# Gate and up by Strassen's scheme, down as a second phase, in an encoder block with two FFNs

## The chip, the cores and the metric

One core of one Trainium2 chip runs the whole kernel. Its time is the device time of one execution in microseconds (us), the median of several runs.

## The reference

One layer of a hybrid encoder over 1280 tokens (1024 of one request, 256 of another), width 1024:

```
x = x + 0.5 * post1(SwiGLU_1(pre1(x)))        # FFN 1
h = pre2(x);  p = h @ w_in
A = bidirectional RWKV-7(p);  B = grouped-query attention(p)
x = x + post2((sigmoid(gA)*(A @ w_branch_a) + sigmoid(gB)*(B @ w_branch_b)) @ w_out)
x = x + 0.5 * post3(SwiGLU_2(pre3(x)))        # FFN 2
swiglu(h) = (silu(h @ w_gate) * (h @ w_up)) @ w_down     # 1024 -> 2816 -> 1024
```

Every pre and post is an RMSNorm. The RWKV part has small low-rank (LoRA) projections for decay and gate, of 64 rows for each of two directions.

## The kernel before

Everything is kept with full-precision products: an operand is split into a high part (the value cast to the matmul's type) and a low part (the rest), and a product is three matmuls, high x high, high x low, low x high. `split` (L134) does this with one ScalarE cast (L140) and one VectorE subtraction (L141).

The stages in order: FFN 1, the combined projection with attention and the RWKV preparation, the RWKV loop, the two branch projections, the output projection (`gx2`, L1226), FFN 2.

An FFN runs in `ffn` (L169). `pre` (L98) has normalised the tokens, transposed them on TensorE (L121, L123) and split them into `hT`, in three chunks of 512, 512 and 256 tokens. For each of 22 blocks of 128 hidden columns, `wtile` (L143) loads the gate block (512 KB) and splits it, `projT` (L155, matmul L165) multiplies it with all chunks (24 matmuls a chunk: 8 depth steps by 3), ScalarE applies Silu (L178); the same for the up block, VectorE multiplies (L187) and the product is split. After two such blocks their part of the down projection is made: for each of 10 token tiles and 2 halves of the output, 6 matmuls (L206) into a PSUM bank, which VectorE adds to an accumulator `acc` in SBUF (L211; the first time ScalarE copies, L209). After the last block every tile goes through `post` (L289: a product with the gain on GpSimd, L293, the scale and residual on VectorE, L295).

A tile framework puts the instructions of each engine in an order of its own: it walks the program by priority (program order) and simulated times, gives out tile slots of each tag as they come free, and sets the semaphores. On the chip each engine then runs its own list in order. All DMAs are issued from SyncE's queue.

In the RWKV preparation `prep` (L562 on) makes, for each of 4 column groups, 5 chunks of 256 tokens and 2 directions, two pairs of matmuls (L576, L577): the high part of a LoRA weight at full height of 128 rows, and its low part at 64 rows, those of the direction.

Of the kernel before, what the change touches and what calls it, by code (L numbers as in the profile page):

```python
# [7 lines left out]
F32 = mybir.dt.float32  # L8
# [23 lines left out]
LT = 9  # L32
HK = 1
AH = (3, 3, 3)
FB = {"t5": 5, "d4": 6, "dg": 6}
DV = [(1, 4, 7), (3, 7, 9), ()]


class K:
# [57 lines left out]

    def pre(self, W, st, ps, gcol, get_x, ptag, ahead=AH, dve=(), weights=None, normed=False):  # L98

        nc = self.nc  # L100
        out, got = [], []
        for ci, (c0, n) in enumerate(CH):
            h = self.htile(ci)
            xs = []
            for t in range(c0 // 128, (c0 + n) // 128):
                while len(got) < min(TT, ORD.index(t) + 1 + ahead[ci]):
                    got.append(get_x(ORD[len(got)]))
                x = got[ORD.index(t)]
                if normed:
                    xs.append((x, None))  # L110
                    continue

                sq = W.tile([128, D], BF16, name="sq", tag="t5") if ORD.index(t) in dve else None
                dg = W.tile([128, 128], F32, name="dg", tag="dg")
                nc.scalar.activation(out=dg, in_=self.ident, func=AF.Copy, scale=self.rstd(st, x, dve=sq))
                xs.append((x, dg))
            for k in range(KD):
                p = ps.tile([128, 512], F32, name="ptr", tag=ptag)
                for j, (x, dg) in enumerate(xs):
                    if dg is None:  # L120
                        nc.tensor.transpose(p[:, j * 128:(j + 1) * 128], x[:, k * 128:(k + 1) * 128], self.ident)  # L121
                        continue
                    nc.tensor.matmul(p[:, j * 128:(j + 1) * 128], lhsT=x[:, k * 128:(k + 1) * 128], rhs=dg, start=True, stop=True)  # L123
                gk = self.par[:, gcol + k:gcol + k + 1]
                nc.scalar.activation(out=h[:, 0, k], in_=p[:, :n], func=AF.Copy, scale=gk)
                nc.vector.scalar_tensor_tensor(out=h[:, 1, k], in0=p[:, :n], scalar=gk, in1=h.bitcast(F32)[:, 0, k],
                                               op0=ALU.mult, op1=ALU.subtract)
            out.append(h)
            if weights is not None and ci == HK:

                self.ready = self.wtile(weights)
        return out

# [35 lines left out]
    def ffn(self, W, ps, hT, wgu, wd, acc, G=2):  # L169
        nc = self.nc  # L170
        group = []
        for f in range(NF):
            gh, gl = self.wtile(wgu[f, 0])
            sg = W.tile([128, NT], F32, name="sg", tag="t5")

            def eg(ci, p):
                c0, n = CH[ci]
                nc.scalar.activation(out=sg[:, c0:c0 + n], in_=p[:, :n], func=AF.Silu)  # L178
            self.projT(ps, gh, gl, hT, "gu", eg)
            uh, ul = self.wtile(wgu[f, 1])  # L180
            ah = W.tile([128, NT], F32R, name="ah", tag="t5")
            al = W.tile([128, NT], F32R, name="al", tag="t5")

            def eu(ci, p):
                c0, n = CH[ci]
                s = slice(c0, c0 + n)
                nc.vector.tensor_tensor(out=sg[:, s], in0=sg[:, s], in1=p[:, :n], op=ALU.mult)  # L187
                self.split(ah[:, s], al[:, s], sg[:, s])
            self.projT(ps, uh, ul, hT, "gu", eu)
            raw = W.tile([128, D], F32, name="draw", tag="d4")  # L190
            nc.sync.dma_start(out=raw, in_=wd[f * 128:(f + 1) * 128])
            dh = W.tile([128, D], F32R, name="dh", tag="d4")
            dl = W.tile([128, D], F32R, name="dl", tag="d4")
            self.split(dh, dl, raw)
            group.append((ah, al, dh, dl))
            if len(group) == G or f == NF - 1:
                first = f < G
                for t in ORD:
                    ts = slice(t * 128, t * 128 + 128)
                    for hf in range(2):  # L200
                        hs = slice(hf * 512, hf * 512 + 512)
                        p = ps.tile([128, 512], F32, name="pd", tag="dn")
                        i, m = 0, 3 * len(group)
                        for (a_h, a_l, d_h, d_l) in group:
                            for a, b in ((a_h, d_h), (a_h, d_l), (a_l, d_h)):
                                nc.tensor.matmul(p, lhsT=a[:, ts], rhs=b[:, hs], start=i == 0, stop=i == m - 1)  # L206
                                i += 1
                        if first:
                            nc.scalar.copy(acc[:, t, hs], p)  # L209
                        else:  # L210
                            nc.vector.tensor_tensor(out=acc[:, t, hs], in0=acc[:, t, hs], in1=p, op=ALU.add)  # L211
                group = []
        return acc
# [74 lines left out]

    def post(self, W, st, y, gbc, half, xres, late=False):  # L289

        nc = self.nc
        yg = W.tile([128, D], F32, name="yg", tag="d4")
        (nc.vector if late else nc.gpsimd).tensor_tensor(out=yg, in0=y, in1=gbc, op=ALU.mult)  # L293
        r = self.rstd(st, y, half)
        nc.vector.scalar_tensor_tensor(out=y, in0=yg, scalar=r, in1=xres, op0=ALU.mult, op1=ALU.add)  # L295
# [85 lines left out]
class Rwkv:  # L381
# [43 lines left out]
    def prep_weights(self, q, W):  # L425
# [9 lines left out]
        lo = W.tile([128, 2, 128], F32R, name="llo")  # L435
        for d in range(2):
            rs = slice(64 * d, 64 * d + 64)
            nc.vector.tensor_tensor(out=lo[rs], in0=raw[rs, d], in1=hi.bitcast(F32)[rs, d], op=ALU.subtract)
# [121 lines left out]
    def prep(self, q, got, ci, W, ps):  # L560
# [10 lines left out]
        for d in range(2):  # L571
            ds_ = slice(64 * d, 64 * d + 64)
# [485 lines left out]
def build(tc, I, O):  # L1058
    nc = tc.nc
    k = K(tc, I, O)  # L1060
    with tc.tile_pool(name="cst", bufs=1) as cp, tc.tile_pool(name="dr", bufs=1, space=DRAM) as dr, \
# [10 lines left out]
        xs = dr_tiles(dr)  # L1072

# [238 lines left out]
```

## Time and profile before

| what | value |
|---|---|
| median of 3 runs | 3557.58 us (3556.7 to 3557.88) |
| profiled execution | 3558.98 us, its span 3557.2 us |
| TensorE busy | 3467.9 us, 97% |
| VectorE, ScalarE, GpSimd busy | 48%, 36%, 11% |
| granted TensorE clock, mean | 0.988 |
| DMA, mean | 74 GB/s |

A profile line names line, engine, operation, `out<-in`, shape and count. TensorE's matmuls are pipelined: the time of one on a line is longer than the distance to the next, so the distance from start to start (the pitch) is what a matmul costs in a stream. A bracket at the end of a line says how long the engine was idle before it and what released it. Windows list busy times of the engines in a stretch, with the share of the clock that was granted, the share of DMA time in use, and GB/s.

### The profile page before, as it was taken

The numbers are of one execution on the slowest core, as the hardware profiler recorded it, in microseconds if no ns is written. First come the engines' busy times: TensorE is split into PE (matmuls) and PEld (weight loads), VectorE is DVE, ScalarE is ACT, GpSimd is POOL, SyncE is SP. The second block draws the span as 40 slices with busy tenths as digits, with TensorE's granted clock in tenths as the row PEclk, the third lists the DMA queues.
The fourth block names the chain that finished last, engine by engine and source line by source line (L and its number), as shares of the span: only waits on it lengthen the run. The fifth ranks groups of instructions, "written<-read, shape, count | busy, mean of one in ns | idle before, by whom it ended". The sixth has DMA issues, their size and how long they took to land. (4 is left out here: it accounts for less than half of the span.)

```text
span 3557.2 us, 56074 instructions
## 1 busy us (share of the span) xinstructions
PE 3467.9 (97%) x22608; PEld 2907.8 (82%) x22608; DVE 1720.8 (48%) x3300; ACT 1291.6 (36%) x2524; POOL 376.7 (11%) x706
## 2 busy tenths in 40 slices
PE   8999999999899999999989999998999999999997
PEld 7888888888788888887768888888878888888886
DVE  3233333333726776648777667647332333333335
ACT  4211111111523666746556666623432111111112
POOL 0000000000301000003144444410000000000002
PEclk9999999999999999999999999999999999999999
DMA  3111111111324121224352212147221111111103
GB/s 127 42 36 36 36 48 36 42 36 35 131 83 135 59 73 45 84 77 154 130 184 85 70 54 76 41 146 236 102 83 36 42 36 36 36 45 39 36 30 119
DMA packets 155108, 264.93 MB, mean 74 GB/s; under 512 B 16864, under 2 KB 98016, under 8 KB 154720
## 3 DMA queue, kind: packets, MB, share of 16 engines
q1 hardware_dynamic: 154848, 261.34, 22.9%
q8 instruction: 178, 2.92, 0.3%
q14 instruction: 82, 0.67, 0.1%
HBM read 183.94 MB, written 74.06 MB: 73 GB/s over the span
## 5 line engine op out<-in xcount | busy, mean ns | idle before, releaser
L165 PE MATMUL pp<-hT,whi 128*128 128x512 f32 (+1 forms) x6000 | 1643.1, 360 | 7.8 <-ACT qk L950 4.9
L165 PEld LDWEIGHTS pp<-hT,whi 128*128 128x128 f32 x6000 | 1068.0, 190 | 175.6 <-ACT qk L950 5.7
L165 PE MATMUL pp<-hT,wlo 128*128 128x512 f32 (+1 forms) x3000 | 1074.4, 358 | 0.0
L165 PEld LDWEIGHTS pp<-hT,wlo 128*128 128x128 f32 x3000 | 569.3, 190 | 79.8
L141 DVE TENSOR_TENSOR wlo<-wraw,whi 128x1024 fp32r<-128x1024 f32 x125 | 154.1, 1233 | 566.7 <-ACT whi L140 566.6
L211 DVE TENSOR_TENSOR acc<-acc,pd 128x512 f32<-128x512 f32 x400 | 271.3, 685 | 203.4 <-PE pd L206 203.2
L206 PE MATMUL pd<-dh,ah 128*128 128x512 f32 x880 | 346.4, 394 | 13.8 <-DVE acc L211 13.8
L206 PE MATMUL pd<-dh,al 128*128 128x512 f32 x880 | 345.6, 393 | 0.0
L206 PE MATMUL pd<-dl,ah 128*128 128x512 f32 x880 | 345.4, 392 | 0.0
L293 POOL TENSOR_TENSOR yg<-acc,gb 128x1024 f32<-128x1024 f32 x19 | 48.2, 2544 | 2075.1 <-DMA xb<-x_d 1128.6
L723 ACT CAST tt<-inv 128x512 f16<-128x512 f32 x400 | 226.6, 588 | 90.7 <-PE inv L721 66.4
L187 DVE TENSOR_TENSOR sg<-sg,pp 128x512 f32<-128x512 f32 x132 | 79.0, 598 | 347.8 <-PE pp L165 347.8
L140 ACT CAST dh<-draw 128x1024 fp32r<-128x1024 f32 x44 | 46.0, 1046 | 528.8 <-DMA draw<-wd 528.8
L140 ACT CAST ah<-sg 128x512 fp32r<-128x512 f32 x132 | 72.2, 547 | 439.5 <-DVE sg L187 439.5
L206 PEld LDWEIGHTS pd<-dh,ah 128*128 128x128 f32 x880 | 166.7, 189 | 52.0 <-DVE acc L211 18.1
L717 DVE TENSOR_TENSOR y<-inv,lv 128x256 f16<-128x256 f32 x400 | 161.6, 418 | 83.6 <-PE inv L715 61.4
L140 ACT CAST whi<-wraw 128x1024 fp32r<-128x1024 f32 x125 | 131.1, 1049 | 194.1 <-PE pp L165 191.7
L206 PEld LDWEIGHTS pd<-dh,al 128*128 128x128 f32 x880 | 166.7, 189 | 35.3
L206 PEld LDWEIGHTS pd<-dl,ah 128*128 128x128 f32 x880 | 166.6, 189 | 33.8
L178 ACT ACTIVATE sg<-pp 128x512 f32<-128x512 f32 x132 | 69.1, 524 | 327.1 <-PE pp L165 325.8
L1156 PE MATMUL pbr<-yT,whi 128*128 128x256 f32 x640 | 124.1, 291 | 19.2 <-ACT yT L140 8.9
L720 PE MATMUL inv<-y,tt 128*128 128x128 f16 x800 | 130.7, 221 | 0.0
(228 smaller groups left out, 4868.3 us busy)
## 6 DMA issues: line engine op xcount, KB each, us to landing
wraw<-wgu SPq DMA_DIRECT2D x88, 512.0 KB, 3.5
draw<-wd SPq DMA_DIRECT2D x44, 512.0 KB, 3.8
gate_d<-go SPq DMA_DIRECT2D x16, 640.0 KB, 3.2
ar_d<-ar SPq DMA_DIRECT2D x40, 256.0 KB, 2.1
bk_d<-bk SPq DMA_DIRECT2D x40, 256.0 KB, 2.1
AR<-ar_d SPq DMA_DIRECT2D x80, 128.0 KB, 2.9
BK<-bk_d SPq DMA_DIRECT2D x40, 256.0 KB, 2.9
g<-gate_d SPq DMA_DIRECT2D x80, 128.0 KB, 3.3
```

Of the source, the lines that this page charges most:

```text
L140: self.nc.scalar.copy(dst_h, src)
L141: self.nc.vector.tensor_tensor(out=dst_l, in0=src, in1=dst_h.bitcast(F32), op=ALU.subtract)
L165: nc.tensor.matmul(p[:, :n], lhsT=a[:, ks], rhs=h[:, b, k], start=i == 0, stop=i == 23)
L178: nc.scalar.activation(out=sg[:, c0:c0 + n], in_=p[:, :n], func=AF.Silu)
L187: nc.vector.tensor_tensor(out=sg[:, s], in0=sg[:, s], in1=p[:, :n], op=ALU.mult)
L206: nc.tensor.matmul(p, lhsT=a[:, ts], rhs=b[:, hs], start=i == 0, stop=i == m - 1)
L211: nc.vector.tensor_tensor(out=acc[:, t, hs], in0=acc[:, t, hs], in1=p, op=ALU.add)
L293: (nc.vector if late else nc.gpsimd).tensor_tensor(out=yg, in0=y, in1=gbc, op=ALU.mult)
L717: nc.vector.tensor_tensor(out=y1, in0=m, in1=mask(l), op=ALU.mult)
L720: nc.tensor.matmul(dbl[:, h, 0], lhsT=tt[:, h, 1], rhs=y1[:, h], start=True, stop=True)
L723: nc.scalar.copy(tt, dbl)
L1156: nc.tensor.matmul(p, lhsT=a[:, ks], rhs=ys[ci][:, b, kk], start=i == 0, stop=i == 11)
```

## The change

FFNs. Two hidden blocks f and f+1 (as rows of the transposed product) by the two halves of the depth form a 2x2 block matrix A, the tokens of the first two chunks by the two halves of the depth a 2x2 matrix B. `columns2` computes the four blocks of the product with 7 products of half depth instead of 8; the 256 tokens of the third chunk (`T`) are computed as before. `second_chunk` makes the combinations T1 to T4 of B once per FFN and splits them; S1 to S4 of A are made and split for each pair and each of gate and up. Operands are in a ring of 6 slots (`opr`). The product silu(gate)*up is written to DRAM (`a_d`). `down` then runs in three groups of tiles (4, 4 and 2), each with its accumulators in PSUM through all 22 blocks: for every block and group it loads the activations and both halves of the down weights again, and splits them. `ends` scales straight from PSUM, with no GpSimd. For the first pair, what needs no combination is done first for gate and up (`early`), with its four weight blocks loaded twice. In FFN 2 the output projection takes the tiles in the order of `PRE` and interleaves the first and third chunk's transposes.

LoRA. The low part of a weight is kept at 128 rows for each direction, the other 64 set to zero on GpSimd. The tile `go` moves to the tag `w1`, of which there are 3 slots.

```diff
-FB = {"t5": 5, "d4": 6, "dg": 6}
+FB = {"t5": 3, "w2": 8, "sc": 5, "x1": 2, "dg": 6}
+YB = {"y": 8, "op": 3}
+GRP = ((0, 1, 2, 3), (4, 5, 6, 7), (8, 9))
+PRE = (0, 1, 2, 3, 8, 9, 4, 5, 6, 7)
...
+    def second_chunk(self, W, ps, xs, gcol):
+        nc = self.nc
+        for k in range(4):
...
+            self.turn(p12, xs, k)
+            self.turn(p22, xs, k + 4)
...
+            o = self.slot("B22", k)
+            self.hilo(o[:, 0], o[:, 1], p22, g4)
+            b12 = W.tile([128, 512], F32, name="b12", tag="sc")
+            nc.scalar.activation(out=b12, in_=p12, func=AF.Copy, scale=g0)
+            t3 = W.tile([128, 512], F32, name="t3", tag="sc")
+            nc.vector.scalar_tensor_tensor(out=t3, in0=p22, scalar=g4, in1=b12, op0=ALU.mult, op1=ALU.subtract)
+            o = self.slot("T3", k)
+            self.split(o[:, 0], o[:, 1], t3)
+            o = self.slot("B11", k).bitcast(F32)
+            t1 = W.tile([128, 512], F32, name="t1", tag="sc")
+            nc.vector.tensor_tensor(out=t1, in0=o[:, 0], in1=o[:, 1], op=ALU.add)
+            nc.vector.tensor_tensor(out=t1, in0=b12, in1=t1, op=ALU.subtract)
...
+    def opr(self, src, n=512):
+        i = self.nop % len(self.ring)
+        self.nop += 1
+        pool, tag = self.ring[i]
+        o = pool.tile([128, 2, 512], F32R, name="op", tag=tag)
+        self.split(o[:, 0, :n], o[:, 1, :n], src)
+        return o
...
+    def prod(self, out, o, rhs, start, stop):
+        i = 0
+        for k in range(4):
+            ks = slice(k * 128, k * 128 + 128)
+            for a, b in ((0, 0), (0, 1), (1, 0)):
+                self.nc.tensor.matmul(out, lhsT=o[:, a, ks], rhs=rhs(k, b), start=start and i == 0, stop=stop and i == 11, skip_group_check=True)
+                i += 1
+    def columns2(self, W, ps, wgu, f, j, sg, hT, bank=None, early=False):
...
+        A = self.blocks(W, w, ("A11", "A12", "A21", "A22"))
+        o = self.opr(A["A11"])
+        self.prod(X, o, comb("B11"), True, True)
+        nc.scalar.copy(x1, X)
+        self.prod(T[:, :256], o, tail(0), True, False)
+        o = self.opr(A["A12"])
+        self.prod(T[:, :256], o, tail(1), False, True)
+        direct(0, slice(1024, NT), T[:, :256])
+        self.prod(X, o, comb("B21"), False, True)
+        direct(0, slice(0, 512), X)
+        o = self.opr(A["A21"])
+        self.prod(T[:, 256:], o, tail(0), True, False)
+        if early:
...
+            yield
+            A = self.blocks(W, w, ("A11", "A12", "A21", "A22"))
+        S = {n: W.tile([128, 512], F32, name="w2", tag="w2") for n in ("S1", "S2", "S3", "S4")}
...
+        self.prod(Y, self.opr(S["S2"]), comb("T2"), True, True)
+        nc.vector.tensor_tensor(out=u, in0=x1, in1=Y, op=ALU.add)
+        self.prod(Z, self.opr(S["S1"]), comb("T1"), True, True)
+        nc.scalar.copy(p5, Z)
+        self.prod(V, self.opr(S["S3"]), comb("T3"), True, True)
+        nc.vector.tensor_tensor(out=v, in0=u, in1=V, op=ALU.add)
+        self.prod(Z, self.opr(S["S4"]), comb("B22"), False, True)
+        nc.vector.tensor_tensor(out=c12, in0=u, in1=Z, op=ALU.add)
...
+        o = self.opr(A["A22"])
+        if not early:
+            self.prod(T[:, 256:], o, tail(1), False, True)
+            direct(1, slice(1024, NT), T[:, 256:])
+        self.prod(V, o, comb("T4"), False, True)
+        nc.vector.tensor_tensor(out=c22, in0=v, in1=p5, op=ALU.add)
+        nc.vector.tensor_tensor(out=c21, in0=u, in1=V, op=ALU.add)
...
+    def down(self, W, ps, wd, a_d, tiles):
+        nc, n = self.nc, 128 * len(tiles)
+        bk = [[ps.tile([128, 512], F32, name="pd", tag="mm") for _ in range(2)] for _ in tiles]
         for f in range(NF):
...
+            tag = ("w2", "sc")[f % 2]
+            ar = W.tile([128, 512], F32, name="ar", tag=tag)
+            nc.sync.dma_start(out=ar[:, :n], in_=a_d[f][:, tiles[0] * 128:tiles[0] * 128 + n])
+            a = self.opr(ar[:, :n], n)
+            d = []
+            for hf in range(2):
+                raw = W.tile([128, 512], F32, name="draw", tag=tag)
+                nc.sync.dma_start(out=raw, in_=wd[f * 128:(f + 1) * 128, hf * 512:hf * 512 + 512])
+                d.append(self.opr(raw))
+            for i in range(len(tiles)):
+                ts = slice(i * 128, i * 128 + 128)
+                for hf in range(2):
+                    for m, (x, y) in enumerate(((0, 0), (0, 1), (1, 0))):
+                        nc.tensor.matmul(bk[i][hf], lhsT=a[:, x, ts], rhs=d[hf][:, y], start=f == 0 and m == 0, stop=f == NF - 1 and m == 2)
+    def ends(self, W, WY, st, bk, tiles, gb, xres, put):
+        for i, t in enumerate(tiles):
+            y = WY.tile([128, D], F32, name="y", tag="y")
+            for hf in range(2):
+                hs = slice(hf * 512, hf * 512 + 512)
+                nc.vector.tensor_tensor(out=y[:, hs], in0=bk[i][hf], in1=gb[:, hs], op=ALU.mult)
+            ys.append((y, self.rstd(st, bk[i], True)))
+        for t, (y, r) in zip(tiles, ys):
...
+            nc.vector.scalar_tensor_tensor(out=y, in0=y, scalar=r, in1=x, op0=ALU.mult, op1=ALU.add)
+            nc.sync.dma_start(out=put(t), in_=y)
...
-        lo = W.tile([128, 2, 128], F32R, name="llo")
+        lo = W.tile([128, 2, 2, 128], F32R, name="llo")
...
-                nc.tensor.matmul(p[:, j], lhsT=lo[ds_, j], rhs=src[ds_, d, cs], start=False, stop=True)
+                nc.tensor.matmul(p[:, j], lhsT=lo[:, d, j], rhs=src[:, d, cs], start=False, stop=True)
...
-        o = W.tile([128, n], F32, name="go", tag="go")
+        o = W.tile([128, n], F32, name="go", tag="w1")
...
+                    for i, ts in enumerate(GRP):
+                        bk = k.down(W, ps, I["wd"][0], a_d, ts)
+                        if i == 2:
+                            norm2(1)
+                        y = k.ends(W, WY, st, bk, ts, gb, k.xin, lambda t: x1_d[t * 128:(t + 1) * 128])
+                        ys.update(zip(ts, y))
+                        if i == 1:
+                            norm2(0)
+                    k.ready = k.wtile(I["watt"][5])
+                    norm2(2)
```

`norm2` normalises and transposes a chunk of FFN 1's output for the projection that follows. `B11` and `B21` are the first chunk's halves, `B22` the second's lower half; `prod` is one product of half depth (12 matmuls).

## Rows read from the trace of the kernel before

**Rows 1.** Page, part 1: busy us, share of the span, instructions.
```profile
PE 3467.9 (97%) x22608; PEld 2907.8 (82%) x22608; DVE 1720.8 (48%) x3300; ACT 1291.6 (36%) x2524; POOL 376.7 (11%) x706
```

**Rows 2.** Windows, FFN 1's steady stretch: length, engines' busy us, clock, DMA share, GB/s.
```profile
200.00:800.00 600.00, 600.00 (x2976) 510.49 (x2975) 198.84 (x271) 90.99 (x134) 0.00 (x0) 1.00 0.12 39
```

**Rows 3.** Timeline of TensorE in both FFNs: start, us, line, count.
```profile
852.00 0.39 PE L206 MATMUL pd<-dl,ah 128*128 128x512 f32 x1
852.68 0.39 PE L206 MATMUL pd<-dl,ah 128*128 128x512 f32 x1
...
866.79 0.62 PE L165 MATMUL pp<-hT,whi 128*128 128x512 f32 x2
...
867.47 0.40 PE L165 MATMUL pp<-hT,whi 128*128 128x256 f32 x2
...
867.82 0.40 PE L165 MATMUL pp<-hT,whi 128*128 128x256 f32 x2
...
3500.04 0.63 PE L165 MATMUL pp<-hT,whi 128*128 128x512 f32 x2
...
3500.74 0.63 PE L165 MATMUL pp<-hT,whi 128*128 128x512 f32 x2
```

**Rows 4.** Groups by line and form, 0 to 870 us, VectorE and ScalarE.
```profile
L141 DVE TENSOR_TENSOR al<-sg,ah 128x512 fp32r<-128x512 f32 x40 | 27.7, 692 | 27.4 <-ACT ah L140 27.4
L126 DVE SCALAR_TENSOR_TENSOR hT<-ptr,par,hT 128x512 fp32r<-128x512 f32 x16 | 11.0, 744 | 3.8 <-ACT hT L125 3.8
...
L140 ACT CAST ah<-sg 128x512 fp32r<-128x512 f32 x40 | 24.8, 620 | 195.5 <-DVE sg L187 195.5
L125 ACT ACTIVATE hT<-ptr,par 128x512 fp32r<-128x512 f32 x16 | 9.9, 687 | 0.2
```

**Rows 5.** Timeline of TensorE, FFN 1: first product, last group, transposes, projection.
```profile
22.49 0.50 PE L165 MATMUL pp<-hT,whi 128*128 128x512 f32 x1
...
925.10 0.39 PE L206 MATMUL pd<-dh,al 128*128 128x512 f32 x1
...
950.26 2.04 PE L123 MATMUL ptr<-dg,acc 128*128 128x128 f32 x16
...
980.22 0.73 PE L165 MATMUL pp<-hT,whi 128*128 128x512 f32 x2 [1.08 <-DVE hT L126]
```

**Rows 6.** Timeline of VectorE at the ends of both FFNs.
```profile
941.69 3.46 DVE L295 SCALAR_TENSOR_TENSOR acc<-yg,r,xb 128x1024 f32<-128x1024 f32 x1
...
3552.31 1.28 DVE L295 SCALAR_TENSOR_TENSOR acc<-yg,r,xb 128x1024 f32<-128x1024 f32 x1
```

**Rows 7.** Timeline of TensorE from the output projection into FFN 2.
```profile
2597.48 1.91 PE L121 MATMUL ptr<-ident,x 128*128 128x128 f32 x16
...
2610.92 1.22 PE L165 MATMUL pp<-hT,whi 128*128 128x512 f32 x2 [1.08 <-DVE hT L126]
```

**Rows 8.** Windows with heavy transfers: the start, and the branch projections.
```profile
0.00:20.00 20.00, 10.80 (x64) 10.25 (x64) 8.34 (x24) 13.87 (x30) 0.20 (x4) 1.00 0.91 344
...
2400.00:2440.00 40.00, 32.10 (x241) 30.29 (x241) 25.55 (x55) 13.20 (x24) 0.00 (x0) 0.96 0.83 250
2440.00:2500.00 60.00, 55.97 (x372) 50.51 (x370) 41.60 (x100) 21.87 (x48) 0.00 (x0) 0.97 0.77 241
```

**Rows 9.** DMA issues by line: count, KB each, us to landing.
```profile
wraw<-w_out SPq DMA_DIRECT2D x16, 256.0 KB, 3.5
...
g_d<-go SPq DMA_DIRECT2D x20, 128.0 KB, 1.9
```

**Rows 10.** Timeline of TensorE in the RWKV preparation, LoRA matmuls.
```profile
1577.92 0.28 PE L165 MATMUL pp<-hT,wlo 128*128 128x256 f32 x1
1578.04 0.28 PE L576 MATMUL pl<-low,lhi 128*128 128x256 f32 x1
1578.25 0.38 PE L577 MATMUL pl<-low,llo 64*128 64x256 f32 x1
1578.56 0.39 PE L576 MATMUL pl<-low,lhi 128*128 128x256 f32 x1
```

**Rows 11.** Windows, the densest stretch of the RWKV preparation.
```profile
1700.00:1750.00 50.00, 50.00 (x248) 38.79 (x247) 44.51 (x98) 35.82 (x78) 14.04 (x33) 1.00 0.49 165
```

More of the change, by code (lines that the diff above doesn't have):

```diff
@@ L96, in htile @@
         return self.hp.tile([128, 2, KD, n], F32R, name="hT", tag=f"h{n}")
[L98 to L132, printed above, removed]
     def split(self, dst_h, dst_l, src, half=False):
@@ L167, in projT @@
             emit(ci, p)
-    def ffn(self, W, ps, hT, wgu, wd, acc, G=2):
-        nc = self.nc
-        group = []
-        for f in range(NF):
[L173 to L213, printed above, removed]
@@ new lines, in slot, with xsrc @@
+    def slot(self, c, k):
+        if c in ("B11", "B21"):
+            return self.hA[:, 4 * (c == "B21") + k]
+        i = 5 * k + ("B22", "T3", "T1", "T2", "T4").index(c)
+        if i < 8:
+            return self.hB[:, i]
+        if 12 <= i < 16:
+            return self.hE[:, i - 12]
+        if i not in self.late:
+            self.late[i] = self.xp.tile([128, 2, 512], F32R, name="hX", tag="x")
+        return self.late[i]
+    def xsrc(self, W, st, x, normed, dve=False):
+        if normed:
+            return x, None
+        sq = W.tile([128, D], BF16, name="sq", tag="t5") if dve else None
+        dg = W.tile([128, 128], F32, name="dg", tag="dg")
+        self.nc.scalar.activation(out=dg, in_=self.ident, func=AF.Copy, scale=self.rstd(st, x, dve=sq))
+        return x, dg
@@ new lines, in turn, with hilo @@
+    def turn(self, p, xs, k):
+        for j, (x, dg) in enumerate(xs):
+            o, i = p[:, j * 128:(j + 1) * 128], x[:, k * 128:(k + 1) * 128]
+            if dg is None:
+                self.nc.tensor.transpose(o, i, self.ident)
+            else:
+                self.nc.tensor.matmul(o, lhsT=i, rhs=dg, start=True, stop=True)
+    def hilo(self, h, l, p, gk):
+        nc = self.nc
+        nc.scalar.activation(out=h, in_=p, func=AF.Copy, scale=gk)
+        nc.vector.scalar_tensor_tensor(out=l, in0=p, scalar=gk, in1=h.bitcast(F32), op0=ALU.mult, op1=ALU.subtract)
@@ new lines, in opr, with blocks @@
+    def opr(self, src, n=512):
[5 more added lines that the diff above has]
+        return o
+    def blocks(self, W, w, which):
+        out = {}
+        for n in which:
+            out[n] = W.tile([128, 512], F32, name="w2", tag="w2")
+            c = 512 * (int(n[2]) - 1)
+            self.nc.sync.dma_start(out=out[n], in_=w[int(n[1]) - 1][:, c:c + 512])
+        return out
@@ new lines, in gate_up @@
+    def gate_up(self, W, ps, wgu, a_d, hT, bank):
+        for f in range(0, NF, 2):
+            sg = [W.tile([128, NT], F32, name="sg", tag="t5") for _ in range(2)]
+            parts = [self.columns2(W, ps, wgu, f, j, sg, hT, bank if f == j == 0 else None, f == 0) for j in range(2)]
+            if f == 0:
+                for p in parts:
+                    next(p)
+            for p in parts:
+                for _ in p:
+                    pass
+            for i in range(2):
+                self.nc.sync.dma_start(out=a_d[f + i], in_=sg[i])
@@ L1072, in build @@
         xs = dr_tiles(dr)
+        a_d = dr.tile([NF, 128, NT], F32, name="a_d")
         with tc.tile_pool(name="hp", bufs=1, side="right") as hp, tc.tile_pool(name="wp", bufs=2, side="right") as k.wp:
             k.hp = Bufs(hp, {"h512": 2, "h256": 1})
-            with tc.tile_pool(name="acc", bufs=1) as k.accp, tc.tile_pool(name="W", bufs=1) as W0, tc.tile_pool(name="ps", bufs=4, space=PSUM) as ps:
+            k.ring = [(k.wp, t) for t in ("wraw", "whi", "wlo")] * 2
+            k.nop = 0
+            with tc.tile_pool(name="W", bufs=1, side="right") as W0, tc.tile_pool(name="ps", bufs=8, space=PSUM) as ps:
@@ L1266, in lay_out @@
+            late.close()
 def lay_out(v):
```

193 lines of the change are left out of this document (138 added, 55 removed).

## The prediction

> **What bounds the kernel now.** I read the page's first part first: TensorE is busy for 97% of the span, no other engine for half of it [rows 1]. Then the windows: in FFN 1's steady stretch TensorE is busy for 600 of 600 us at full clock, VectorE for a third, DMA for 12% [rows 2]. So there the end is set by the number of matmuls times their pitch, and the timeline gives the pitch: three matmuls of 512 columns take 867.47-866.79 = 0.68 us (0.2267 each) in FFN 1, three of 256 take 0.35 to 0.36 us (0.12), the down matmuls again 0.68 for three, while gate and up in FFN 2 take 0.70 for three (0.2333) [rows 3]. An FFN has 2x22x2x24 = 2112 gate and up matmuls of 512 columns, 1056 of 256, and 22x60 = 1320 down matmuls. That makes 3432x0.2267 + 1056x0.12 = 904.7 us for FFN 1 and 492.7 + 126.7 + 299.2 = 918.6 us for FFN 2. The stretches are longer: FFN 1 lasts from 0 to 980.2 [rows 5], FFN 2 from the end of the output projection at 2597.5 [rows 7] to the span's end at 3557.2, 959.7 us. So 75.5 and 41.1 us are overhead, at the edges. Of FFN 1's, 22.5 us pass before the first product, 30.0 us (950.3 to 980.2) while the output is transposed, and the last 48 down matmuls take 25.2 us (925.1 to 950.3) where 10.9 would do [rows 5]. There VectorE's residual step takes 3.46 us beside GpSimd's product; the same step takes 1.28 us where GpSimd is idle [rows 6].
>
> **The change part by part.**
>
> *Products.* For a pair of blocks and one of gate and up, 84 matmuls of 512 columns stand for 96; the 48 of 256 stay. 22 such pairs save 264 matmuls: 264x0.2267 = 59.8 us in FFN 1, 264x0.2333 = 61.6 us in FFN 2. Down keeps its 1320. The minimum becomes 844.9 and 857.1 us.
>
> *Pitch.* Why FFN 2's gate and up run at 0.2333 no row shows. The moving operands now lie in other buffers, so either pitch is possible: 1848x0.0067 = 12.3 us each way per FFN. Twelve of the 20 slots of T1 to T4 and B22 are new places; I add 3 us in FFN 1 and nothing in FFN 2 (bounds -12 to +12 in each).
>
> *Cover in the gate and up phase.* One pair now takes 84x0.2267 + 48x0.12 = 24.8 us of TensorE. VectorE has 8 split subtractions, 4 combinations S, 5 additions, and up to 5 products for up: 17x0.69 = 11.7 us for gate, 15.3 us for up, about 54% on average; ScalarE has 8 casts (0.62), 2 copies and the Silus, some 9 us [rows 4]. Both fit. The waits are the question: an eviction (x1, p5, v) must be done before the next product goes into the same bank. Between lie at least one half-depth product, 12x0.2267 = 2.7 us, or two tail products of 1.4 us, and an eviction takes 0.6 to 0.7 us. The ring of 6 slots lets splits run about five operands, over 10 us, ahead. What an eviction can be late by is the work queued on its engine, two to four steps of 0.7 us. Before, no such wait showed in this stretch [rows 2]. Bounds 0 to 2 us per pair, 0 to 44 us per FFN; I take the end by the nearest row (no stall), with a little on top: 5 us per FFN. Write-out of `a_d` (2 x 640 KB per 50 us) lies under the 12% of DMA [rows 2].
>
> *Prologue.* Each of the 4 steps of `second_chunk` gives VectorE 11 operations, 3 from PSUM at 0.744 and 8 at 0.692 us = 7.8 us, 31.1 us in all; ScalarE 2x0.687 + 4x0.62 = 3.9 us, 15.4 in all, beside it [rows 4]. With 8 splits of weights (5.5 us) that is 36.6 us of VectorE before the last combination is there. TensorE has as cover the early part, 2x(24x0.2267 + 48x0.12) = 22.4 us, and three of four depth steps of the five other products, 45x0.2267 = 10.2 us, together 32.6 us of FFN work, if the order takes them as they become ready. In FFN 1 the second chunk can start at about 27 us (the first product of before at 22.5 [rows 5], and the third chunk's eight hi/lo pairs of some 0.5 us that now come ahead), ends at about 63, and TensorE has then done 32.6 us of its minimum: overhead 30 us. In FFN 2 the last tile's normalisation takes about 7 us after 2597.5 (squares of both banks and of the row, two roots, the scale; no row shows the chain as a whole), so the combinations end at 2641: 43.6 - 32.6 = 11 us of overhead, against the 13.4 us that lay between [rows 7]. Bounds: no cover by the 45 matmuls, +10 each; cover of everything, -10 each.
>
> *Down as a phase.* The additions into `acc` (VectorE) go; they were hidden. Per block a group of four tiles takes 24x0.2267 = 5.4 us of TensorE, with 3 splits (2.1 us of VectorE, 1.9 of ScalarE) and 768 KB of transfers, 145 GB/s. That is below the 241 GB/s that a window with 128 KB transfers shows [rows 8], so it is hidden by a lookahead of about four blocks in 13 raw slots. The third group takes 12x0.2267 = 2.7 us per block with 640 KB, 241 GB/s, and beside it lie the residual reads and result writes of the second group (about 4 MB in its 60 us): 18.6 MB at 60 us are 310 GB/s. The start moved 344 GB/s at 0.91 of the engines, a stretch with short rows 250 at 0.83, so 301 at full use [rows 8]: the third group is at the edge. VectorE has 22x1.8 = 40 us there plus 10.6 us of `ends`, and in FFN 1 about 12 us for two `norm2` chunks: 62 of 60. I take +5 us in FFN 1 and +4 in FFN 2 (bounds 0 to 17: 18.6 MB at 241 GB/s take 77 us). Turning from gate and up to down: the last banks must be evicted and `a_d` of the last pair is far behind the reads of block 0, 3 and 2 us. Between groups the eight banks are evicted at 0.69 us each, while 3 matmuls (0.68 us) refill each: some 1.5 us a boundary, 3 us an FFN.
>
> *Edges.* After FFN 1 only the two tiles of the third group are left: 4 evictions, the root, two scale steps of 1.28, a second root, 16 transposes and 8 hi/lo pairs of 256 columns, 14 us (bounds 5, if the projection's first chunk fills it, to 25), in place of the 30 us and of the slow last group. After FFN 2: 0.69 + 1.2 for the small operations + 2x1.28 + the 3.6 us from the last step of before to the end [rows 6] = 8 us; there the whole of what lies between 918.6 + 13.4 and 959.7 goes, 27.7 us.
>
> *LoRA.* A stream of 256-column matmuls has a pitch of 0.12 us. The 64-row matmul starts 0.21 us after the 128-row one, and the next starts 0.31 us after it [rows 10]. 80 such pairs cost 0.52 us each where two full matmuls would cost 0.24: 22 us of TensorE. It is full in that stretch, but VectorE follows at 44.5 of 50 us [rows 11], so a part may not come through; and `go` now takes one of three `w1` slots until its write has landed, 1.9 us, 20 times [rows 9], up to +38 us if the chain behind waited each time. I take -15 (bounds -22 to +16). The memsets on GpSimd are 8 small ones on an engine with 14 of 50 us in use.
>
> The Trainium skill speaks against this edit: by TensorEngine Tiling (Tiling Modes, Key Properties) different tiles of the array can load and multiply in parallel, so half-height matmuls of two directions could share the array, and full height would forfeit that. By that rule the edit would save nothing. The rows show no such overlap, 0.31 us where a full matmul takes 0.12 [rows 10]; the sum goes by the rows.
>
> *Sum.* FFN 1: 844.9 + 3 + 5 + 30 + 3 + 3 + 5 + 14 = 907.9 for 980.2, -72.3. FFN 2: 857.1 + 5 + 11 + 2 + 3 + 4 + 8 = 890.1 for 959.7, -69.6. LoRA -15. The span becomes 3557.2 - 156.9 = 3400.3 us; the execution had 1.8 us around its span, and the median of the runs lies 1.4 us below the profiled time of 3558.98. That gives 3400.7, say 3401 us.
>
> **The rivals.**
>
> *A. Transfers set the pace of the third group.* At the 241 GB/s of the busiest short-row stretch [rows 8] 18.6 MB take 77 us, 17 more per FFN against 5 and 4 in the sum: 3401 + 25 = 3426. For it: 310 GB/s is asked. Against: the start reached 344.
>
> *B. VectorE sets the prologue and little covers it.* If TensorE's order leaves the early part where it stands but none of the 45 matmuls ahead, and the combinations start 10 us later: +20 per FFN, 3441. For it: 36.6 us of VectorE against 22.4 of sure cover.
>
> *C. Slower than before: evictions queue ahead of splits.* If in each pair five products had to wait until an eviction (0.7 us), a cast (0.62) and a subtraction (0.69) had run one after another, with hand-over some 1.8 us each less what lies ready, 1.3 to 1.8: 44 pairs x 5 x 1.5 = 330 us, 3401 + 330 = 3731, slower than before by 173. It decides from 157/44 = 3.6 us of waiting per pair. Against: before, the next weight's cast stood ahead of the Silu that it followed in the program, and TensorE had no gap [rows 2].
>
> *D. Transfers of the down phase come one at a time.* A 256 KB transfer lands in 3.5 us [rows 9]; three in series take 10.5 us where 5.4 are there, and the third group waits too: 44x5.1 + 22x7 = 378 us per FFN, over 4100 in all. Against: 241 GB/s with 128 KB each [rows 8], which no series at 3.5 us gives. The Trainium skill's rule to batch transfers to 1 MiB (DMA: Bandwidth & Descriptors, Bandwidth) points the same way; by its fit of 2.0 us plus bytes at 436 GB/s (Anatomy of one DMA), an estimate, three in series would take 7.8 us and the loss would be 2x200 us. The rows show transfers side by side.
>
> *E. All goes to the good bounds:* pitch 0.2267 in FFN 2, no stalls, the projection fills the transition: 3401 - 12 - 10 - 9 - 9 = 3361.
>
> **How the numbers follow.** Forecast 0.54 (its own range 3380 to 3420), A 0.14, B 0.17, C 0.05, D 0.02, E 0.07; 0.01 for no change. A and B together would give 3466. The range runs from 3362 to 3472, leaving C, D and about half of E's chance out. What a measurement of this kernel can tell from no change is 0.2%, 7 us. Faster by more: 0.92; within it 0.01; slower 0.07 (C and D).
>
> **What would show it.** Right: 528 matmuls of 512 columns fewer in the two FFNs, a period of about 24.8 us per pair with TensorE full, three steps of down of 120, 120 and 60 us, a LoRA pitch of 0.12, and the projection's first product at about 908. Wrong: gaps on TensorE after S splits or evictions within a pair (C), a third group over 70 us with raw tiles as the releaser (A), FFN 1's first product with T2 later than 75 us (B). The forecast is wrong as a whole if the saving per pair is less than the 2.7 us of one product.

## The result, and the profile after

The changed kernel takes 3441.14 us (median of 4 runs, 3438.6 to 3442.5) against 3557.14 us of the kernel before (4 runs, 3554.99 to 3557.88) in the same comparison: 0.9674 of it, 95% interval 0.9657 to 0.9691. That is 116 us less, inside the range, where 157 was forecast. The profiled execution's span is 3440.7 us for 3557.2, 116.5 less.

The page's first part (busy us, share of the span, instructions) answers to [rows 1]:

```profile
PE 3332.3 (97%) x22080; PEld 2797.2 (81%) x22080; DVE 1997.9 (58%) x3909; ACT 1572.7 (46%) x3116; POOL 333.3 (10%) x695
```

TensorE has the 528 matmuls fewer and is still busy for 97%. VectorE has 277 us more work.

Windows (length, busy us of PE, PEld, DVE, ACT, POOL, clock, DMA share, GB/s) of the start, of both steady stretches and of the RWKV preparation answer to [rows 2, 11]:

```profile
40.00:50.00 10.00, 10.00 (x67) 9.17 (x66) 10.00 (x17) 7.99 (x15) 0.00 (x0) 1.00 0.01 2
50.00:60.00 10.00, 8.11 (x49) 6.96 (x49) 10.00 (x18) 5.89 (x11) 0.00 (x0) 1.00 0.00 0
...
100.00:500.00 400.00, 400.00 (x2087) 340.69 (x2086) 208.15 (x319) 118.77 (x198) 0.00 (x0) 1.00 0.20 67
...
1650.00:1700.00 50.00, 46.55 (x256) 37.88 (x257) 46.24 (x100) 35.96 (x78) 19.60 (x35) 1.00 0.50 165
...
2600.00:3000.00 400.00, 400.00 (x2066) 338.68 (x2065) 212.25 (x326) 121.35 (x203) 0.00 (x0) 1.00 0.21 72
```

In the steady stretches TensorE has no gap at all with VectorE at 52%. The start is another matter: VectorE is busy for 10 of 10 us in both of its rows, while TensorE, still full in the first, has 8.11 of 10 us in the second. In the preparation TensorE, which was full, now has gaps, and VectorE stands at 46 of 50.

The timeline of TensorE (start, us, line, count, idle before and its releaser) through FFN 1 answers to [rows 5]:

```profile
36.66 3.00 PE L247 MATMUL X<-hA,op 128*128 128x512 f32 x12
...
59.32 3.14 PE L247 MATMUL T<-hT,op 128*128 128x256 f32 x24 [1.89 <-DVE sg L262]
65.16 1.09 PE L247 MATMUL V<-hB,op 128*128 128x512 f32 x2 [2.71 <-ACT op L105]
...
845.73 9.69 PE L169 MATMUL ptr<-dg,y 128*128 128x128 f32 x64 [6.26 <-ACT dg L159]
855.18 3.02 PE L352 MATMUL pd<-op 128*128 128x512 f32 x12
...
915.85 7.30 PE L169 MATMUL ptr<-dg,y 128*128 128x128 f32 x64
928.90 5.46 PE L169 MATMUL ptr<-dg,y 128*128 128x128 f32 x32 [5.75 <-ACT dg L159]
935.45 0.72 PE L130 MATMUL pp<-hT,whi 128*128 128x512 f32 x2 [1.08 <-DVE hT L174]
```

The first product starts at 36.7 us (22.5 before), the five other products run steadily from 66, and the combined projection starts at 935.45 where it started at 980.22: FFN 1 gives 44.8 us. Before the third down group TensorE waits 6.26 us and transposes for 9.69; after it come 64 transposes, a wait of 5.75 us and 32 more. The group itself takes 60.8 us.

The same view into and inside FFN 2 answers to [rows 3, 7]:

```profile
2555.85 1.09 PE L167 MATMUL ptr<-ident,xt 128*128 128x128 f32 x8 [3.93 <-ACT xt L1419]
2559.82 1.22 PE L247 MATMUL X<-hA,op 128*128 128x512 f32 x2 [2.88 <-ACT op L105]
...
2569.14 3.35 PE L247 MATMUL X<-hA,op 128*128 128x512 f32 x7 [3.19 <-DVE op L106]
...
2710.89 1.56 PE L247 MATMUL Z<-hB,op 128*128 128x512 f32 x6
2712.29 0.86 PE L247 MATMUL Z<-hE,op 128*128 128x512 f32 x3
```

The first product comes at 2559.8 but runs steadily only from 2569.1. The pitch of 512 columns is 1.40/6 = 0.2333 us again. FFN 2 lasts from 2549.3, the output projection's last matmul, to 3440.7: 891.4 us for 959.7, 68.3 less.

The LoRA matmuls answer to [rows 10]:

```profile
1565.67 0.28 PE L725 MATMUL pl<-low,lhi 128*128 128x256 f32 x1
1565.79 0.28 PE L726 MATMUL pl<-low,llo 128*128 128x256 f32 x1
1565.91 0.62 PE L130 MATMUL pp<-hT,whi 128*128 128x512 f32 x2
```

Each costs 0.12 us, where a pair cost 0.52. But from the first to the last of them pass 219.1 us (1533.3 to 1752.4) for 225.4: 6 us less, where 15 were forecast.

### The profile page after: what moved, and what is told of

It reads as the page before. It is cut to its first block, busy times and chain, and to the rows that moved or that the text cites. A ratio compares the mean times of both kernels' runs of the same rounds, so it can differ in the third digit from the quotient of the medians.

```text
span 3440.7 us, 58121 instructions
## 1 busy us (share of the span) xinstructions
PE 3332.3 (97%) x22080; PEld 2797.2 (81%) x22080; DVE 1997.9 (58%) x3909; ACT 1572.7 (46%) x3116; POOL 333.3 (10%) x695
## 5 line engine op out<-in xcount | busy, mean ns | idle before, releaser
L352 PE MATMUL pd<-op 128*128 128x512 f32 x2640 | 604.2, 391 | 0.9 <-DVE op L106 0.9
L352 PEld LDWEIGHTS pd<-op 128*128 128x128 f32 x2640 | 495.0, 188 | 109.4 <-DVE op L106 1.3
L130 PE MATMUL pp<-hT,whi 128*128 128x512 f32 (+1 forms) x1776 | 501.9, 362 | 6.9 <-ACT qk L1099 5.1
L106 DVE TENSOR_TENSOR op<-w,op 128x512 fp32r<-128x512 f32 x356 | 245.1, 691 | 275.0 <-ACT op L105 273.2
L130 PEld LDWEIGHTS pp<-hT,whi 128*128 128x128 f32 x1776 | 315.3, 192 | 46.5 <-ACT qk L1099 5.9
L130 PE MATMUL pp<-hT,wlo 128*128 128x512 f32 (+1 forms) x888 | 319.9, 360 | 0.0
L247 PEld LDWEIGHTS T<-hT,op 128*128 128x128 f32 x2112 | 271.0, 190 | 15.6 <-DVE sg L262 2.3
L247 PE MATMUL T<-hT,op 128*128 128x256 f32 x2112 | 274.4, 283 | 3.2 <-DVE sg L262 1.9
L247 PE MATMUL X<-hA,op 128*128 128x512 f32 x1056 | 262.3, 397 | 7.7 <-DVE op L106 3.2
L130 PEld LDWEIGHTS pp<-hT,wlo 128*128 128x128 f32 x888 | 169.8, 191 | 19.0
```

Of the source, the lines that this page charges most:

```text
L106: self.nc.vector.tensor_tensor(out=dst_l, in0=src, in1=dst_h.bitcast(F32), op=ALU.subtract)
L130: nc.tensor.matmul(p[:, :n], lhsT=a[:, ks], rhs=h[:, b, k], start=i == 0, stop=i == 23)
L247: self.nc.tensor.matmul(out, lhsT=o[:, a, ks], rhs=rhs(k, b), start=start and i == 0, stop=stop and i == 11, skip_group_check=True)
L352: nc.tensor.matmul(bk[i][hf], lhsT=a[:, x, ts], rhs=d[hf][:, y], start=f == 0 and m == 0, stop=f == NF - 1 and m == 2)
```

## The experiments

Each was timed against the kernel before, which had medians from 3555.75 to 3556.83 us in these comparisons. The changed kernel, at 3441.14, is the other reference.

**Eight products instead of seven, the rest of the change kept.** What is Strassen's scheme worth by itself? X, Y, Z and V take two direct products each, and the combinations S1 to S4, T1, T2 and T4 are not made.

```diff
-self.prod(X, o, comb("B11"), True, True)
-nc.scalar.copy(x1, X)
+ops = [o]
+self.prod(X, o, comb("B11"), True, False)
...
+o = self.opr(A["A22"])
+self.prod(T[:, 256:], o, tail(1), False, True)
```

> Eight direct half-depth products instead of seven, no combinations of either side, everything else (down as a second phase, a_d in DRAM, LoRA) as in the changed kernel. Theory 1, gate and up are bound by TensorE and nothing else: 528 matmuls more at 0.2333 cost 123 us, and the prologues without combinations give back 20 to 35 us: 3441 becomes 3530 to 3545. Theory 2, evictions and splits on VectorE already eat part of the saving within the pairs: less than 60 us more, under 3500.

It took 3548.38 us (3544.18 to 3552.93), 0.9978 of before [0.9969, 0.9988], just above the first theory's interval. So the scheme carries 107 of the 116 us, its combinations at the start included, and the new phases and the LoRA edit together some 8.

**Operands shifted by 32 bytes.** Why is the pitch 0.232 to 0.2333 and not 0.2267? A small tile ahead of the pools X, Y and hp shifts what lies in them.

```diff
-with tc.tile_pool(name="X", bufs=1) as XP:
+with tc.tile_pool(name="shx", bufs=1) as SH, tc.tile_pool(name="X", bufs=1) as XP:
+    nc.vector.memset(SH.tile([128, 8], F32, name="shift"), 0.0)
...
```

> Empty tiles of 32 bytes ahead of the pools on the left shift the moving operands of both FFNs and of the output projection, so that the moving and the stationary operand of each of these matmuls start at the same address modulo 128 bytes; nothing else changes. Theory 1, the pitch hangs on where the two operands lie against each other: gate and up fall from 0.2333 to about 0.228 us per matmul of 512 columns in FFN 2 (1848 matmuls, -10 us) and from 0.231 in FFN 1 (-7 us), the output projection and down give some 5 us more: 3441 becomes 3415 to 3425. Theory 2, the pitch hangs on what else runs (VectorE, transfers): 0.2333 stays and so does 3441.

3432.24 us (3424.97 to 3437.21), 0.9656 [0.964, 0.9672]: between the theories. Six V matmuls in FFN 2 still took 1.39 to 1.40 us. I then worked out from the addresses that the program gives its tiles where moving and stationary operand of each matmul begin. Modulo 512 bytes the two lie 160 bytes apart in all gate and up products of 512 columns in the changed kernel's FFN 2, and 128 bytes apart with the pad; the pitch there was 0.233 to 0.235 us and 0.230 to 0.236 us, by product. The clearest case is the changed kernel's output projection, whose two halves of the weights take turns: 0.228 us for the half with equal offsets, 0.234 for the one 160 bytes apart. In the kernel before, gate and up had equal offsets in FFN 1 (0.2267) and 160 bytes between them in FFN 2 (0.2333) [rows 3].

In FFN 1 of the changed kernel only the operands in `hX` and `hE` lie 160 bytes off, while those in `hA` and `hB` have equal offsets. Yet six products from `hB` take no less time than six from `hX`:

```profile
588.44 1.55 PE L247 MATMUL V<-hB,op 128*128 128x512 f32 x6
589.83 1.57 PE L247 MATMUL V<-hX,op 128*128 128x512 f32 x6
```

1.39 us for six are 0.232 each. So equal offsets of a matmul's own operands are not enough where its neighbours' differ.

**Operands at equal offsets.** The pads become 160 bytes, which makes the offsets equal modulo 512 for all matmuls of 512 columns in both FFNs and in the output projection.

```diff
-nc.vector.memset(SH.tile([128, 8], F32, name="shift"), 0.0)
+nc.vector.memset(SH.tile([128, 40], F32, name="shift"), 0.0)
...
```

> The empty tiles ahead of the left pools are 160 bytes instead of 32, so that moving and stationary operand of every 512-column matmul of both FFNs and of the output projection start at the same address modulo 512 bytes. In the profiled executions before, matmuls with that property had a pitch of 0.227 to 0.229 us and all others 0.232 to 0.234, and the 32 bytes had moved most gate and up operands from one wrong offset to another. Theory 1, the offset modulo 256 or 512 sets the pitch: all of them come to 0.227 to 0.229, gate and up save 1848 x 0.005 = 9 us in FFN 2 and 6 in FFN 1, the output projection and down some 4: 3441 becomes 3418 to 3424. Theory 2, the offset goes along with something else: pitch 0.2325 as with 32 bytes and 3432.

3417.28 us (3414.68 to 3418.53), 0.9607 [0.9594, 0.962], 24 below the changed kernel and 1 below the range of the first theory. Timeline and windows of this kernel:

```profile
2699.84 1.52 PE L247 MATMUL V<-hB,op 128*128 128x512 f32 x6
2701.20 1.52 PE L247 MATMUL V<-hX,op 128*128 128x512 f32 x6
```

```profile
100.00:500.00 400.00, 400.00 (x2128) 346.32 (x2127) 209.35 (x320) 121.58 (x202) 0.00 (x0) 1.00 0.20 69
2600.00:3000.00 400.00, 400.00 (x2118) 345.88 (x2118) 210.29 (x322) 121.76 (x203) 0.00 (x0) 1.00 0.20 70
```

Six matmuls take 1.36 us, also those from `hB` in FFN 1, whose own offsets had been equal before, and 400 us hold 41 and 52 matmuls more than in the changed kernel. Against the run before, nothing but addresses had changed. The half of the output projection that was 160 bytes off goes from 0.234 to 0.227. In FFN 1 the gate and up phase ends at 590.0 us for 598.3.

**The first normalisation inside the third down group,** after 5 of its 22 blocks instead of ahead of it.

```diff
-bk = k.down(W, ps, I["wd"][0], a_d, ts)
+bk = k.down(W, ps, I["wd"][0], a_d, ts, (lambda: norm2(0)) if i == 2 else None)
...
-if i == 1:
-    norm2(0)
...
+if hook and f == 4:
+    hook()
```

> The normalisation and transposes of FFN 1's first chunk are put after the fifth block of the third down group instead of ahead of the group. Theory 1, the 15.7 us between the second and third group are a matter of order: the 6.3 us of waiting for the first diagonal tile go and the transposes run at 7.3 us instead of 9.7: 3441 becomes 3431 to 3435. Theory 2, VectorE and ScalarE are full in the third group, so the work only moves: gaps appear within the group and the time stays at 3441 (3438 to 3444).

3433.96 us (3432.74 to 3435.9), 0.9656 [0.9642, 0.9671]: the first theory. Its timeline of TensorE:

```profile
845.67 9.02 PE L352 MATMUL pd<-op 128*128 128x512 f32 x38 [0.66 <-DVE op L106]
854.53 7.31 PE L169 MATMUL ptr<-dg,y 128*128 128x128 f32 x64
...
928.57 0.73 PE L130 MATMUL pp<-hT,whi 128*128 128x512 f32 x2 [1.08 <-DVE hT L174]
```

The wait of 6.26 us has become 0.66, and the projection starts 6.9 us earlier. The transposes themselves stay on the path.

**Fewer additions in the prologue,** T4 like T1: the low parts of the first chunk's operands are left out of both.

```diff
-nc.vector.tensor_tensor(out=t1, in0=o[:, 0], in1=o[:, 1], op=ALU.add)
-nc.vector.tensor_tensor(out=t1, in0=b12, in1=t1, op=ALU.subtract)
+nc.vector.tensor_tensor(out=t1, in0=b12, in1=o[:, 0], op=ALU.subtract)
...
```

> Leaves out the low parts of the first chunk in T1 and T4, which takes 8 VectorE additions (0.69 us each, 5.5 us) out of each FFN's prologue. Theory 1, the prologue is set by VectorE's queue: each FFN starts full work 5 us earlier, 3441 becomes 3429 to 3433. Theory 2, the prologue is set by the last tile's normalisation and by TensorE's own order (all transposes ahead of the first products): 3 us or less in all, 3438 to 3441.

3435.31 us (3432.22 to 3438.01), 0.9659 [0.9645, 0.9674]: between the theories. In FFN 1 Y's run began at 61.87 us for 66.05, so there VectorE sets the start. In FFN 2 the gate and up phase took 579.6 us for 580.0, so there these additions are not what decides.

**FFN 2's first weight buffers in a pool of their own.** In the changed kernel SyncE issues them at 2555.82, after ScalarE's last `xt` (L1419) has ended at 2555.80: their pool overlaps the output rows `wo`.

```diff
-W = Bufs(W0, FB)
+W = Bufs(W0, FB, Bufs(WA, {"w2": 8, "x1": 2}))
...
```

> In FFN 2 the weight blocks (w2, x1) get a pool of their own, over the memory of the output projection's first half of weights alone, which is free 5 us before the projection ends; in the changed kernel they share a pool whose other tiles lie over the last output rows. Theory 1, the pool's opening waits for the last row's normalisation and so holds the first weight loads back to 2556: with a pool of their own they start at about 2544, the early products begin at the end of the projection and FFN 2 gains 6 to 10 us: 3431 to 3435. Theory 2, VectorE's queue of combinations sets the prologue of FFN 2 whatever the loads do: 3438 to 3441.

3439.42 us (3436.89 to 3441.59), 0.967 [0.9657, 0.9683]: the second theory. The loads were issued at 2542.21, but on TensorE's timeline

```profile
2556.13 1.97 PE L167 MATMUL ptr<-ident,xt 128*128 128x128 f32 x8 [5.04 <-ACT xt L1419]
2557.75 3.89 PE L247 MATMUL X<-hA,op 128*128 128x512 f32 x12
...
2589.87 0.79 PE L247 MATMUL Y<-hB,op 128*128 128x512 f32 x1 [5.97 <-DVE op L106]
```

the last tile's transposes stand ahead of X and wait for it 5.04 us, and at Y it waits 5.97 us more, for VectorE. Of 13 us 2 come through: the gate and up phase takes 577.9 us for 580.0.

**The LoRA edit taken apart.** First half height again, with `go` left on the ring `w1`; then both undone.

```diff
-nc.tensor.matmul(p[:, j], lhsT=lo[:, d, j], rhs=src[:, d, cs], start=False, stop=True)
+nc.tensor.matmul(p[:, j], lhsT=lo[ds_, j], rhs=src[ds_, d, cs], start=False, stop=True)
...
```

> The changed kernel with the LoRA low weights back at 64 rows; the tile go stays on w1. Theory 1, TensorE's 22 us in that stage are worth what the trace shows, most of them lost to VectorE and to waits within the preparation: 3444 to 3450. Theory 2, they are worth the 15 us of the prediction and something else made the stage longer: 3454 to 3460.

```diff
-o = W.tile([128, n], F32, name="go", tag="w1")
+o = W.tile([128, n], F32, name="go", tag="go")
```

> As the run before, and go on a tag of its own again: the whole LoRA edit undone, the FFNs as changed. If the shared w1 slots held the preparation up, this is faster than the run before by 3 us or more; if not, it is the same within 2 us. The edit as a whole is worth the difference to 3441: 6 us by the trace of the stage (3447), 15 by the prediction (3456).

Half height took 3457.97 us (3451.91 to 3460.31), 0.9718 [0.9704, 0.9731], the second theory; both undone 3446.21 us (3441.81 to 3451.04), 0.969 [0.9677, 0.9703]. So full height is worth 17 us with `go` on `w1`, `go` on `w1` costs 12 at half height, and the edit as a whole is worth 5, by medians whose runs scatter over 4 to 9 us.

**`go` on another ring,** in the kernel with three edits together (below).

```diff
-o = W.tile([128, n], F32, name="go", tag="w1")
+o = W.tile([128, n], F32, name="go", tag="ak")
```

> As the run with three edits together, and the gate copy `go` of the LoRA products takes its buffer from the ring `ak` (5 takers of 3 buffers a step) in place of `w1` (4 takers of 3). Theory 1 (the 12 us that `go` was found to cost beside the weights' height are a wait of `w1`'s takers for buffers): 6 to 12 us below that run's 3409, 3397 to 3403. Theory 2 (the place was not the cause: the stage is paced by VectorE, whose `bk` the 12.0 us of ScalarE's waits in it name, or `ak` passes the wait on to its own takers): 3405 to 3415.

3411.78 us (3410.54 to 3417.22), 0.96 [0.9583, 0.9618], against 3409.25 without: the second theory. Waits of ScalarE in the LoRA stretch (waited for, us in total, times, longest), in the kernel with the whole edit undone:

```profile
ACT sao L727 <- PE pl L726: 24.2, 32, 1.6
ACT sao L727 <- DVE bk L761: 2.3, 2, 1.2
```

and in the changed kernel:

```profile
ACT sao L727 <- DVE bk L761: 12.1, 15, 2.1
ACT sao L727 <- PE pl L726: 2.2, 6, 0.7
```

The wait for TensorE's pairs went, and half of it came back as a wait for VectorE. In the kernel with `go` on `ak` it is 10.6 us for VectorE and, though its pairs are at full height, 12.4 for TensorE, with the same 231 us from the first LoRA matmul to the last `pb` as without. So these waits change places and their sum does not give the time. Which of the two rings `go` takes decides nothing at full height; a buffer of its own beside full height was not tried.

**Three edits together:** equal offsets, the normalisation inside the group, the pool of its own.

> The changed kernel with three edits together: every 512-column FFN and output-projection matmul with its moving and stationary operand starting at the same offset modulo 512 bytes, the first normalisation of the second FFN's input issued inside the third down group, and the second FFN's first weight buffers in their own pool. Theory 1 (the three pieces lie in different stretches and add): 3441 - 24 - 7 - 2 = 3406 to 3411 us. Theory 2 (the pieces overlap; with faster matmuls the loads, VectorE or DMA become late instead): 3414 to 3418, no better than the alignment alone.

3409.25 us (3404.51 to 3412.54), 0.9587 [0.9573, 0.9601]: the pieces add.

**The additions of T1 and T4 on GpSimd,** beside the three edits.

```diff
-nc.vector.tensor_tensor(out=t1, in0=o[:, 0], in1=o[:, 1], op=ALU.add)
+nc.gpsimd.tensor_tensor(out=t1, in0=o[:, 0], in1=o[:, 1], op=ALU.add)
...
```

> As the run with three edits together, and the additions T1 and T4 of the first and second chunk go to GpSimd in place of VectorE. Theory 1 (VectorE bounds the start of the first pair: about 5.5 us of additions fewer on it in each prologue): 3 to 8 us below that run, near 3400. Theory 2 (a GpSimd operation holds VectorE while it runs, as the 3.46 against 1.28 us of the rows of L295 would have it): the prologue is as long or longer, so 0 to 5 us above that run.

3407.06 us (3404.79 to 3409.86), 0.9581 [0.9565, 0.9597]: 2 us less, within the spread of both, so not decided by its time. Groups by line, 30 to 60 us, first of this kernel, then with all on VectorE:

```profile
L210 DVE TENSOR_TENSOR t<-b,t 128x512 f32<-128x512 f32 x4 | 4.9, 1227 | 0.0
```

```profile
L210 DVE TENSOR_TENSOR t<-b,t 128x512 f32<-128x512 f32 x4 | 2.8, 692 | 0.0
```

The subtraction that follows takes 1.23 us for 0.69 in the mean: two of the four run beside a GpSimd addition and take 1.76 and 1.78 us, the two others 0.68. Operations that read one operand from PSUM keep their 0.74 us beside GpSimd. This gives back most of the addition that VectorE was spared. The second theory's mechanism is there; its price is no more than the saving.

**The early products ahead of the second chunk's transposes,** in both FFNs, beside the three edits.

```diff
+first = k.first_pair(W, ps, I["wgu"][0], hT, bank)
 k.second_chunk(W, ps, src(range(4, 8)), 0)
-k.gate_up(W, ps, I["wgu"][0], a_d, hT, bank)
+k.gate_up(W, ps, I["wgu"][0], a_d, hT, first)
...
```

> As the run with three edits together, and the first pair's early products are put ahead of the second chunk's transposes in the program's order, so that they stand ahead of them in PE's queue. Theory 1 (in the prologue PE idles because its order puts the transposes of the last tiles ahead of products that are ready): the second FFN's first product starts some 5 us earlier and the whole is 4 to 10 us faster, near 3400. Theory 2 (the prologue's end is set by VectorE's additions and splits of the second chunk, which this delays or leaves): 0 to 4 us from that run on either side.

3418.68 us (3415.59 to 3421.11), 0.9614 [0.96, 0.9628]: 9 us slower than without, outside both theories. Windows of this kernel, then of the one without:

```profile
30.00:40.00 10.00, 10.00 (x66) 9.16 (x66) 5.37 (x8) 5.55 (x10) 0.00 (x0) 0.99 0.24 76
...
60.00:70.00 10.00, 6.97 (x19) 4.17 (x17) 9.28 (x16) 4.73 (x8) 0.00 (x0) 0.83 0.00 0
70.00:80.00 10.00, 7.30 (x19) 4.49 (x20) 9.96 (x17) 4.72 (x8) 0.00 (x0) 0.83 0.01 2
```

```profile
30.00:40.00 10.00, 10.00 (x74) 9.51 (x74) 9.64 (x16) 6.49 (x12) 0.00 (x0) 0.95 0.26 79
...
60.00:70.00 10.00, 7.29 (x31) 5.83 (x31) 8.17 (x15) 2.46 (x4) 0.00 (x0) 0.83 0.32 107
70.00:80.00 10.00, 10.00 (x45) 8.27 (x45) 9.58 (x16) 4.94 (x9) 0.00 (x0) 1.00 0.31 105
```

With the products first, the second chunk's transposes come at 49.94 us, where the changed kernel has them at 27.96:

```profile
49.94 7.31 PE L169 MATMUL ptr<-dg,xt 128*128 128x128 f32 x64
```

So VectorE is half idle from 30 to 40 us; its work moves to 60 to 80 us, where TensorE has only what VectorE lets through, 19 matmuls in each 10 us for 31 and 45. The order of the changed kernel was the better of the two: it feeds the busy engine first.

## Why the prediction was right, and where it was 40 us off

The scheme was right: 264 half-depth matmuls fewer per FFN, no gap in the steady stretch, down as a phase without new waits. By the profiled execution 116.5 us were saved and 156.9 forecast. Term by term, over the same minimum of 844.9 and 857.1 us:

| term | FFN 1: forecast, measured | FFN 2: forecast, measured |
|---|---|---|
| Prologue | 30, 44 | 11, 22 |
| Pitch in gate and up | 3, 8 | 0, 0 |
| Cover (stalls) | 5, 0 | 5, 0 |
| phase change, boundaries, third group, down's pitch | 11, 3 | 9, 4 |
| Edges | 14, 35 | 8, 8 |

FFN 1's gate and up phase ends at 598.3 where its minimum is 545.7: 52.6 us, of which the run at equal offsets takes away 8.3 (590.0), and 44.3 are left for the start. FFN 2's takes 580.0 us for 557.8. The edge of FFN 1 is 15.7 us before the third group (839.5 to 855.2) and 19.4 after it.

**Edges** is the step that failed most, by 21 us. It counted the evictions and 16 transposes of the last two tiles, which with the chain around them took 12.3 us after the other transposes (923.15 to 935.45), near the 14. `norm2` of the other eight was put on VectorE alone, beside the third group. But its transposes (9.69 and 7.30 us) and its wait (6.26) stand in TensorE's queue, and all of it is path: 23.3 us. The transposes could have been counted from the diff; that the wait could be hidden, and they could not, the run with the normalisation inside the group shows.

**Prologue**: 14 and 11 us short. VectorE's time was sized well (it is full from 31.7 to 68 us, 36.3 us for 36.6), its start and the cover were not. In FFN 1 the combinations began at 31.7 us where some 27 was assumed, which is 5 of the 14 us. Of the 45 matmuls that were to run ahead six did, and 39 at 0.2267 us are the other 9. All 64 transposes of the second chunk came before the first product. Rival B had this mechanism. Its total of 3441 is the time measured, but by accident: only 25 of the 40 us come from its place, and its own mark (the first product with T2 after 75 us) was not met, since Y begins at 56.4 and goes on with `hX` at 66.5. The runs with fewer additions and with the early products first show the reason in FFN 1: VectorE sets the end. In FFN 2 the chain of the last tile's normalisation, put at 7 us without a row, took 6.6 (2549.3 to 2555.85), and no single part that was tried sets the end: neither fewer additions (0.4 us) nor loads 13.6 us earlier (2 us) moved it much, as the last tile's chain takes the place of the loads and VectorE that of the chain.

**LoRA**: 5 to 6 us came where 15 were forecast, and the two prices behind it were as in the text: the height is worth 17 us (22 by the rows, if all came through), `go` costs 12 at half height (up to 38). The sum weighed the second too lightly. What paces the stage now is not shown: from 1540 to 1740 us TensorE is busy for 191 and VectorE for 174 of 200 us, and no run takes work off VectorE there; whether the stage would be faster with a place for `go` stays open too. The Trainium skill's rule that tiles of the array work in parallel (TensorEngine Tiling (Array Packing), Tiling Modes, Key Properties) would have had the height save nothing; the 17 us speak against it for this use, where half and full height alternate. The rule beside it in the same list, that a change of the tiling mode drains TensorE, fits the 0.52 us of a pair, where two matmuls of full height cost 0.24; no run tells a drain from another cause.

**Pitch**: the guess of 3 in FFN 1 and 0 in FFN 2 came out as 8 and 0, inside the bounds. What the prediction had left without a row is settled: the run at equal offsets gives 0.2267 in both, and the 0.2333 of FFN 2 before goes with operands 160 bytes apart.

**Cover, third group**: too careful by 23 us in all, which hid part of the rest. Rival C needed 3.6 us of waiting per pair; there is none. Rival A needed 77 us for the third group; it took 60.8. Rival D needed transfers in series; the weights of down land so:

```profile
draw<-wd SPq DMA_DIRECT2D x264, 256.0 KB, 3.3
```

3.3 us each, yet three transfers of 256 KB fit in every 5.4 us, and in the third group (60.8 us for 22 blocks) three in every 2.8, one of them of 128 KB. The fit behind the 7.8 us for three in series stands in the Trainium skill (DMA: Bandwidth & Descriptors, Anatomy of one DMA) for transfers issued by GpSimd, and these are issued by SyncE; nothing in the sum rests on it.

## What to carry to other kernels

When a change saves matmuls, the steady stretch gives what the count says; the loss is at the edges, so list every instruction that the new order puts into the bounding engine's queue there, transposes too, and not only the work of the engine that computes. At a start where the helper engine is full, feed that engine first and let the bounding engine wait. When matmuls of one shape have two pitches, compare the start addresses of their two operands, and of their neighbours': 160 bytes of padding were worth 24 us here, as much as a fifth of the whole change.

## What the runs showed of the hardware that was not expected

- The pitch of a 512-column matmul depends on where its operands lie: 0.2267 us in streams with equal offsets modulo 512 bytes throughout, and 0.230 to 0.236 with 128 or 160 bytes between them. It takes some matmuls to settle: after 256-column matmuls the first five of such a stream come at 0.228 to 0.236 us, so that products of the run at equal offsets average 0.2267 to 0.229. Equal offsets modulo 128 were not enough (the run with 32 bytes); whether modulo 256 would do, and why, these runs do not show.
- A VectorE subtraction of two 128x512 operands in SBUF takes 1.76 to 1.78 us beside a GpSimd addition and 0.68 without, while VectorE operations with one operand in PSUM keep their 0.74 us; the 3.46 against 1.28 us of [rows 6] had shown the same for another operation.
